# A two-layer block of four sequence mixers and a gated ffn: each engine's order set by another model of durations

## The chip, the core and the metric

The kernel runs on one core of a Trainium2 chip. The core has five engines that run side by side, each with an instruction stream of its own that it works through strictly in order: TensorE (PE, matrix multiplication into PSUM; PEld is its loading of weights), VectorE (DVE), ScalarE (ACT), GpSimd (POOL) and SyncE (SP, which here only issues DMAs). An instruction that needs another engine's result waits on a semaphore, and everything behind it on its own engine waits with it. The metric is device time in microseconds, the median of several executions.

## The reference

Two layers over 512 latent tokens and 256 context tokens of width 1024, in fp32. In each layer the tokens are normed and modulated (shift and scale computed from a vector `c` by `mod_w`), projected by `w_in` (3,232 columns), passed through four mixers of 256 columns each, projected by `w_out`, added, normed and modulated again, and passed through a gated ffn of width 2816. The last layer leaves out what only the context's output needs.

```
mod = split(silu(c) @ mod_w[i] + mod_b[i], 6)            # also for c_ctx
h   = modulate(x, norm_mix_g[i], mod[0], mod[1])         # rms norm * (1 + scale) + shift
pa, pb, pc, pd = split(h @ w_in[i])                       # both for x and ctx
oa = rwkv7(pa)      # delta rule: S = S*w + (S a) b^T + v k^T, two directions, 4 heads of 64
ob = diff_attention(pb)   # softmax(q1 k1) - lam * softmax(q2 k2), 4 heads
oc = gla(pc)        # gated linear attention in chunks of 64, two directions, 4 heads
od = gqa(pd)        # 4 query heads on 2 key heads, rope
x  = x + mod[2] * (concat(oa, ob, oc, od) @ w_out[i])
u, g = split(modulate(x, norm_ffn_g[i], mod[3], mod[4]) @ w_up[i])
x  = x + mod[5] * ((silu(conv3(g)) * u) @ w_down[i])
```

## The kernel before

Activations lie as [feature, token] tiles in 30 slabs of SBUF; all matmuls write slices of one PSUM tile named `pst`, so nearly every PE row reads `pst`. Fp32 operands of the large matmuls are split into a rounded part and a rest, and a product is three matmuls: L377 (ACT) rounds, L378 (POOL) subtracts, L387 and L703 multiply (L387 with the weights as the stationary side, giving [feature, token]; L703 with the activations as the stationary side, giving [token, feature]). `projections` (L709) makes all blocks of `w_in` through these two. Every matmul of a projection is independent of the mixers, whose inputs it makes.

The gated linear attention (`gla`, L1100) of one direction takes the cumulated gates (L1114, L1122, L1148, with sums along the tokens as matmuls at L427, the shared helper for transposes and constant products), the scores inside a chunk (L1163), a mask (L1181), the state's products L1186, and the outputs L1197 and L1200; its end on POOL is L1225. The delta rule (`rwkv`, L1260) prepares decays (L1345 to L1376, with L1389 on PE after L1366 on DVE), inverts small triangles (L1418, L1420 on DVE), and runs its chain of chunks (L1545 to L1663). The attentions follow with scores and softmax (L937 to L970; L859 turns the rotated queries).

The modulation is not done on PE alone: `mod_first` (L446) spreads layer 0's shift and scale over PE, DVE (L470) and POOL with ACT (L474, L475), and `mod_part` (L483) does the other 80 blocks of the two layers as 320 products with a sum on DVE (L495), woven into the mixers of layer 0 and into its ffn. A norm takes the mean square (L550), an inverse root by integer steps and three Newton steps on DVE (L400 to L407), a broadcast (L558, L561 on PE), and the scaling L576 and shift L580, whose outputs are the first projections' operands.

The order is set in two steps. `weave` (L300) emits the streams (delta rule, gated linear attention, attentions, projections, modulation) by turns: each has a clock that advances by the number that it yields times a pace, and the stream that is behind goes first. This order of emission gives the instructions their priorities. The framework then fixes each engine's stream with a simulated clock: an engine that comes free takes, of the instructions whose inputs are ready on that clock, the one that was emitted earliest. What it takes for the duration of an instruction, and for the time at which another engine sees a result, so decides which instruction is "ready" when an engine comes free. The resulting streams are fixed in the program; nothing is reordered on the chip.

## Time and profile before

| | us |
|---|---|
| Three runs of the kernel before | 2450.39 median, 2445.48 to 2453.73 |
| Span of the profiled execution | 2445.8 |
| PE busy | 2211.0 (90%) |
| DVE busy | 1490.5 (61%) |
| POOL busy | 1047.3 (43%) |
| ACT busy | 937.5 (38%) |

The page gives no time of the profiled execution beside its span; the span is 4.6 us under the median of the three runs. The span falls into these stretches, by what runs in them: 0 to 92 us the first norm and modulation; 92 to 437 the projections and the gated linear attention of layer 0, with the preparation of the delta rule; 437 to 846 the rest of the delta rule, the attentions and `w_out`; 846 to 1454 the ffn of layer 0, up to 1098 with the modulation of layer 1 on DVE; 1454 to 1517 the norm of layer 1; 1517 to 1830 projections and gated linear attention of layer 1; 1830 to 2026 its delta rule and attentions; 2026 to the end `w_out` and ffn. The granted clock (PEclk) is a share of full speed, averaged over a stretch; it goes between two levels, 2.4 and 1.2 GHz, so that 0.90 in a stretch means that the lower one held a fifth of it.

### The profile page before, as it was taken

How to read it: one execution, taken by the hardware profiler on the slowest of the kernel's cores; microseconds unless marked ns; L12 is line 12 of the kernel's file. 1: busy time of each engine (PE TensorE's matmuls, PEld its weight loads, DVE VectorE, ACT ScalarE, POOL GpSimd, SP SyncE). 2: the span in 40 equal slices, each digit the busy share in tenths (PEclk: the TensorE clock that was granted, in tenths of full speed). 3: DMA queues.
4: the chain of work that ended last, by engine and by line, in shares of the span. 5: the costliest groups of instructions: out<-in, count | busy, mean ns of one | idle time of the engine just before them, and what ended most of it. 6: DMA issues, size and time to landing. Idle time of an engine off the chain costs nothing. (4 is left out here: it accounts for less than half of the span.)

```text
span 2445.8 us, 40328 instructions
## 1 busy us (share of the span) xinstructions
PE 2211.0 (90%) x15292; PEld 1881.8 (77%) x15292; DVE 1490.5 (61%) x3201; ACT 937.5 (38%) x1758; POOL 1047.3 (43%) x1001
## 2 busy tenths in 40 slices
PE   4879898789979998969999999997989889999999
PEld 4767687677857787858888888786878778888888
DVE  6997568678764499994222262367778874423223
ACT  3322222256546342212232344323256564533333
POOL 3442356334221253334343464346433413555556
PEclk9889888799979999989999999898889999999999
DMA  7443134433224334542211142125533232222324
GB/s 250 168 151 119 47 126 121 109 95 84 74 73 139 101 113 148 172 153 70 67 63 61 61 157 70 48 67 148 135 90 83 59 122 95 87 94 95 98 93 138
DMA packets 232434, 259.54 MB, mean 106 GB/s; under 512 B 90992, under 2 KB 174256, under 8 KB 232240
## 3 DMA queue, kind: packets, MB, share of 16 engines
q1 hardware_dynamic: 232240, 256.97, 33.8%
q8 instruction: 120, 1.97, 0.3%
q14 instruction: 74, 0.61, 0.1%
HBM read 210.74 MB, written 37.77 MB: 102 GB/s over the span
## 5 line engine op out<-in xcount | busy, mean ns | idle before, releaser
L387 PE MATMUL pst<-slab,slab 128*128 128x512 f32 (+1 forms) x6552 | 1255.3, 353 | 55.0 <-ACT slab L631 20.8
L387 PEld LDWEIGHTS pst<-slab,slab 128*128 128x128 f32 x6552 | 1065.0, 193 | 239.3 <-ACT slab L631 21.4
L378 POOL TENSOR_TENSOR slab<-slab,slab 128x512 fp32r<-128x512 f32 (+1 forms) x428 | 584.0, 1374 | 728.5 <-ACT slab L377 685.0
L377 ACT CAST slab<-slab 128x512 fp32r<-128x512 f32 (+1 forms) x428 | 257.8, 612 | 538.0 <-PE pst L387 397.5
L703 PE MATMUL pst<-slab,slab 128*128 128x256 f32 (+1 forms) x1872 | 261.8, 302 | 17.9 <-POOL slab L378 17.7
L703 PEld LDWEIGHTS pst<-slab,slab 128*128 128x128 f32 x1872 | 250.4, 205 | 27.8 <-POOL slab L378 19.5
L620 DVE SCALAR_TENSOR_TENSOR slab<-pst,pp,slab 128x511 f32<-128x511 f32 x66 | 41.5, 657 | 312.6 <-ACT slab L617 312.6
L495 DVE SCALAR_TENSOR_TENSOR slab<-slab,slab 128x512 bf16<-128x512 f32 x240 | 227.6, 948 | 6.9 <-DMA slab<-in_modw_dram 0.8
L427 PE MATMUL pst<-cst,slab 128*128 128x128 f32 (+1 forms) x968 | 166.5, 305 | 60.0 <-POOL slab L1148 16.6
L427 PEld LDWEIGHTS pst<-cst,slab 128*128 128x128 f32 (+1 forms) x968 | 121.0, 153 | 88.0 <-DVE slab L859 20.0
L1545 PE MATMUL pst<-slab,slab 128*128 128x128 f32 (+5 forms) x1376 | 162.1, 278 | 9.1 <-DVE slab L1599 4.8
L651 DVE SCALAR_TENSOR_TENSOR slab<-pst,fgate,slab 128x512 f32<-128x512 f32 (+1 forms) x144 | 88.0, 629 | 127.5 <-PE pst L387 127.4
L1545 PEld LDWEIGHTS pst<-slab,slab 128*128 128x128 f32 (+3 forms) x1376 | 135.1, 176 | 29.8 <-issue 14.4
L940 DVE TENSOR_REDUCE mx<-pst 128x1 f32<-128x768 f32 (+1 forms) x120 | 100.2, 846 | 43.3 <-PE pst L937 20.6
L942 ACT ACTIVATE slab<-pst,mx 128x768 f32<-128x768 f32 (+1 forms) x120 | 97.9, 817 | 50.9 <-DVE mx L940 50.1
L632 POOL TENSOR_TENSOR slab<-slab,slab 128x768 fp32r<-128x768 f32 (+1 forms) x44 | 71.2, 1618 | 97.9 <-ACT slab L631 94.4
L626 ACT ACTIVATE slab<-slab 128x768 f32<-128x768 f32 (+1 forms) x44 | 32.4, 737 | 144.2 <-DVE slab L622 144.2
L495 DVE SCALAR_TENSOR_TENSOR slab<-slab 128x512 bf16<-128x512 f32 x80 | 73.5, 918 | 2.3
L1577 POOL TENSOR_TENSOR slab<-slab,pc 128x256 f32<-128x256 f32 x48 | 34.3, 727 | 87.6 <-PE pst L1545 16.0
L953 ACT ACTIVATE slab<-slab,r 128x768 f32<-128x768 f32 (+1 forms) x80 | 67.7, 853 | 8.7 <-DVE r L952 8.1
L970 PE MATMUL pst<-slab,slab 128*64 128x128 f32 x816 | 64.7, 291 | 3.8 <-ACT slab L422 1.7
L631 ACT CAST slab<-slab 128x768 fp32r<-128x768 f32 (+1 forms) x44 | 32.0, 728 | 92.1 <-DVE slab L628 92.0
(309 smaller groups left out, 2689.7 us busy)
## 6 DMA issues: line engine op xcount, KB each, us to landing
slab<-in_wup_dram SPq DMA_DIRECT2D x88, 512.0 KB, 3.4
slab<-in_modw_dram SPq DMA_DIRECT2D x160, 256.0 KB, 2.6
slab<-in_wdn_dram SPq DMA_DIRECT2D x48, 512.0 KB, 3.4
slab<-in_win_dram SPq DMA_DIRECT2D x46, 512.0 KB, 3.6
slab<-in_modw_dram SPq DMA_DIRECT2D x16, 512.0 KB, 7.0
slab<-in_wout_dram SPq DMA_DIRECT2D x16, 512.0 KB, 3.5
slab<-in_xT_dram SPq DMA_DIRECT2D x16, 384.0 KB, 5.7
kb<-slab SPq DMA_DIRECT2D x8, 768.0 KB, 4.2
```

The lines of the kernel that those rows point to most:

```text
L377: nc.scalar.copy(out=w[0], in_=st[:, k:k + q])
L378: nc.gpsimd.tensor_tensor(out=w[1], in0=st[:, k:k + q], in1=w[0].bitcast(F32), op=ALU.subtract)
L387: self.nc.tensor.matmul(ps[:, a:b], w[i][k][:, cols], x[j][k][:, a:b], start=(k == 0 and q == 0), stop=(k == nk - 1 and q == 2))
L427: self.nc.tensor.transpose(out, a.bitcast(F32) if a.dtype != F32 else a, self.c["ident"])
L495: nc.vector.scalar_tensor_tensor(out=junk, in0=w, scalar=1.0, in1=self.sc[s][:, e * hd:(e + 1) * hd], op0=ALU.mult, op1=ALU.mult, accum_ou ...
L632: nc.gpsimd.tensor_tensor(out=HL[:, 1, :n], in0=th[:, :n], in1=HL[:, 0, :n].bitcast(F32), op=ALU.subtract)
L651: nc.vector.scalar_tensor_tensor(out=x[m][:, a:b], in0=ps[:, a:b], scalar=gate[:, m, s:s + 1], in1=x[m][:, a:b], op0=ALU.mult, op1=ALU.add)
L703: self.nc.tensor.matmul(ps[:, :n], h[i][k][:, t * P:(t + 1) * P], w[j][k], start=(k == 0 and q == 0), stop=(k == KD - 1 and q == 2))
L940: nc.vector.tensor_reduce(out=mx, in_=sv, axis=AX.XY, op=ALU.max, negate=True)
L942: nc.scalar.activation(out=p[m][:, a:].rearrange("p (e c) -> p e c", e=2 - a // hb), in_=sv, func=AF.Exp, bias=mx, accum_out=lsum[:, m:m + 1])
L953: nc.scalar.activation(out=p[0][:, a:], in_=p[0][:, a:], func=AF.Copy, scale=r[:, 0:1])
L1545: mm = lambda o, a, b, pos: nc.tensor.matmul(o, a, b, start=True, stop=True, tile_position=pos)
```

## The change

One line changes in the code; the rest of the diff removes comments and docstrings.

```
-    with tile.TileContext(nc) as tc:
+    with tile.TileContext(nc, schedule_with_timeline_sim=True) as tc:
         tile_hybrid_block(tc, A, out)
```

The scheduler's clock then runs on a detailed model of the timeline (what an instruction takes on its engine, and when its result is seen by others) instead of a short table of durations. Every instruction is the same in number, shape and address: 12,488 on PE, 2,869 on DVE, 1,632 on ACT, 1,006 on POOL and 1,073 on SP by the program. Only their order on each engine differs. On PE the two ffn stretches keep their order; the stretches with projections and mixers do not.

The first place is PE in the second direction of the gated linear attention of layer 0. `slab_19_126` to `slab_24_131` are the attention's own tiles; `slab_1_96` to `slab_4_99` and `slab_34` to `slab_41` are operands of the projections. Before:

```order
L387 MATMUL pst<-slab_41_364,slab_4_99 128x512
L387 MATMUL pst<-slab_41_364,slab_4_99 128x256
L1186 MATMUL pst<-slab_19_126,slab_20_127 64x256 x4
L387 MATMUL pst<-slab_34_218,slab_4_99 128x512
L1197 MATMUL pst<-slab_24_131,slab_19_126 64x64 x4
L1200 MATMUL pst<-slab_23_130,slab_19_126 64x64 x4
```

After, the same steps:

```order
L703 MATMUL pst<-slab_4_99,slab_35_236 128x256 x3
L1163 MATMUL pst<-slab_24_131,slab_16_119 32x64 x48
L1186 MATMUL pst<-slab_19_126,slab_20_127 64x256 x2
L703 MATMUL pst<-slab_1_96,slab_36_259 128x256 x3
L703 MATMUL pst<-slab_1_96,slab_37_283 128x256 x3
L703 MATMUL pst<-slab_4_99,slab_34_218 128x256 x3
L703 MATMUL pst<-slab_4_99,slab_35_236 128x256 x3
L703 MATMUL pst<-slab_1_96,slab_36_259 128x256 x3
L703 MATMUL pst<-slab_1_96,slab_37_283 128x256 x3
L1197 MATMUL pst<-slab_24_131,slab_19_126 64x64 x4
L1186 MATMUL pst<-slab_21_128,slab_20_127 64x256 x2
L703 MATMUL pst<-slab_1_96,slab_34_218 128x256
```

The L1186 of this direction stood four in a row between projections at L387, and its L1197 and L1200 followed behind one more matmul. Now it is split into two pairs with eighteen matmuls of L703 between them, and those projections, which stood behind the whole direction, stand ahead of its outputs.

The second place is DVE in the first norm of layer 0: `r` and `t` are the inverse root's tiles, `slab_33_197` at L558 the broadcast that the norm goes on with, and the L470 the modulation's products with their sum into `mod_77`. Before:

```order
L405 TENSOR_TENSOR t_31_182<-r_181 128x6
L406 TENSOR_TENSOR t_31_182<-t_31_182,t_32_183 128x6
L407 SCALAR_TENSOR_TENSOR r_181<-t_31_182,r_181 128x6
L558 TENSOR_TENSOR slab_33_197<-cst,r_181 128x512
L558 TENSOR_TENSOR slab_33_197<-cst,r_181 128x256
L470 SCALAR_TENSOR_TENSOR slab_5_100,mod_77<-slab_17_124,slab_14_113 128x1024
L470 SCALAR_TENSOR_TENSOR slab_5_100,mod_77<-slab_17_124,slab_15_114 128x1024
L576 SCALAR_TENSOR_TENSOR slab_33_197<-slab_8_103,gs_167,slab_33_197 128x512
```

After, with the same Newton steps:

```order
L476 TENSOR_SCALAR mod_77<-mod_77,pp 128x2 x2
L470 SCALAR_TENSOR_TENSOR slab_5_100,mod_77<-slab_21_128,slab_14_113 128x1024
L405 TENSOR_TENSOR t_31_182<-r_181 128x6
L534 SCALAR_TENSOR_TENSOR gs_167<-mod_77,pp 128x2
L470 SCALAR_TENSOR_TENSOR slab_5_100,mod_77<-slab_21_128,slab_15_114 128x1024
L406 TENSOR_TENSOR t_31_182<-t_31_182,t_32_183 128x6
L476 TENSOR_SCALAR mod_77<-mod_77,pp 128x2
L470 SCALAR_TENSOR_TENSOR slab_5_100,mod_77<-slab_24_131,slab_14_113 128x1024
L407 SCALAR_TENSOR_TENSOR r_181<-t_31_182,r_181 128x6
L470 SCALAR_TENSOR_TENSOR slab_5_100,mod_77<-slab_24_131,slab_15_114 128x1024
L873 TENSOR_TENSOR lm_3402<-rows_381 128x64
L405 TENSOR_TENSOR t_31_182<-r_181 128x6
```

Before, L405 to L407 ran without a break up to the broadcast L558, and the L470s stood behind it. Now L470, L476 and L534 stand between the Newton steps; L558 comes further down, and eight L470 more than before stand ahead of it.

The third place is POOL near the end of the gated linear attention of layer 0, ahead of the splits L378 of the weights that L703 takes. L788 copies pieces of projections, L1225 gates the attention's output, L1369 and L1355 belong to the delta rule. Before:

```order
L1225 TENSOR_TENSOR slab_33_197<-slab_33_197,slab_25_132 128x256 x6
L788 TENSOR_TENSOR slab_7_102<-slab_17_124 128x128
L1369 TENSOR_TENSOR slab_23_130<-slab_23_130,slab_16_119 128x768
L1355 COPY pc_56_2045<-slab_21_128 128x12
L788 TENSOR_TENSOR slab_7_102<-slab_17_124 128x128
L378 TENSOR_TENSOR slab_2_97<-slab_7_102,slab_1_96 128x512
L378 TENSOR_TENSOR slab_2_97<-slab_7_102,slab_2_97 128x512
L378 TENSOR_TENSOR slab_3_98<-slab_5_100,slab_3_98 128x512
```

After:

```order
L1369 TENSOR_TENSOR slab_23_130<-slab_23_130,slab_16_119 128x768
L378 TENSOR_TENSOR slab_4_99<-slab_6_101,slab_4_99 128x512
L378 TENSOR_TENSOR slab_1_96<-slab_6_101,slab_1_96 128x512
L378 TENSOR_TENSOR slab_2_97<-slab_7_102,slab_1_96 128x512
L788 TENSOR_TENSOR slab_6_101<-slab_14_113 128x256
L378 TENSOR_TENSOR slab_2_97<-slab_7_102,slab_2_97 128x512
L1225 TENSOR_TENSOR slab_33_197<-slab_33_197,slab_25_132 128x256 x6
L788 TENSOR_TENSOR slab_6_101<-slab_24_131 128x256
```

Before, the six L1225 stood ahead of these L378. Now they stand behind them, and the first two L378 of the upper block (`slab_2_97`) stand further up still.

## Rows read from the trace of the kernel before

**Rows 1.** The page, section 1: busy us, share of the span, instructions.

```profile
PE 2211.0 (90%) x15292; PEld 1881.8 (77%) x15292; DVE 1490.5 (61%) x3201; ACT 937.5 (38%) x1758; POOL 1047.3 (43%) x1001
```

**Rows 2.** Windows: stretch, length; PE, PEld, DVE, ACT, POOL busy; PEclk, DMA, GB/s.

```profile
0.00:92.00 92.00, 52.59 (x196) 44.56 (x196) 70.34 (x133) 35.69 (x62) 39.13 (x25) 0.94 0.58 211
92.00:182.00 90.00, 73.84 (x446) 65.76 (x446) 85.71 (x179) 25.66 (x43) 41.88 (x28) 0.87 0.52 171
182.00:437.00 255.00, 224.71 (x1873) 190.97 (x1874) 176.21 (x397) 67.69 (x132) 119.19 (x109) 0.88 0.34 104
437.00:490.00 53.00, 35.47 (x235) 30.50 (x233) 38.20 (x103) 15.58 (x34) 18.23 (x38) 0.71 0.41 107
490.00:846.00 356.00, 323.92 (x2844) 268.11 (x2844) 236.50 (x602) 191.54 (x413) 102.85 (x154) 0.95 0.31 89
846.00:1098.00 252.00, 215.25 (x1155) 182.57 (x1155) 244.34 (x504) 68.37 (x105) 97.95 (x59) 0.93 0.46 153
1098.00:1454.00 356.00, 356.00 (x2059) 312.17 (x2059) 123.84 (x182) 109.50 (x170) 161.06 (x115) 1.00 0.25 80
...
1517.00:1727.00 210.00, 185.03 (x1561) 156.12 (x1559) 126.46 (x253) 71.94 (x133) 109.03 (x99) 0.91 0.30 90
1727.00:1830.00 103.00, 92.33 (x700) 79.92 (x700) 73.45 (x195) 39.63 (x86) 37.36 (x63) 0.82 0.43 108
1830.00:2026.00 196.00, 180.70 (x1813) 148.40 (x1812) 150.56 (x375) 124.59 (x252) 62.08 (x106) 0.97 0.31 88
```

**Rows 3.** TensorE's waits: us in total, times, the longest.

```profile
PE pst L703 <- POOL slab L378: 17.7, 8, 4.5
PE pst L427 <- POOL slab L1148: 16.6, 4, 8.0
PE pst L427 <- DVE slab L859: 16.5, 9, 8.5
PE pst L1389 <- DVE slab L1366: 14.1, 2, 8.8
...
PE pst L1122 <- DVE slab L1114: 9.9, 1, 9.9
...
PE pst L1186 <- DVE slab L1174: 7.2, 1, 7.2
```

**Rows 4.** Timeline of TensorE, 182 to 277 us: start, us, instruction, idle before.

```profile
187.56 1.54 PE L427 MATMUL pst<-cst,slab 128*128 128x128 f32 x6 [7.96 <-POOL slab L1148]
...
202.98 0.68 PE L1197 MATMUL pst<-slab,slab 64*64 64x64 f32 x8
...
273.55 1.12 PE L1186 MATMUL pst<-slab,slab 128*64 128x256 f32 x4 [7.25 <-DVE slab L1174]
...
275.32 1.11 PE L1197 MATMUL pst<-slab,slab 64*64 64x64 f32 x8
```

**Rows 5.** The page, section 5: one group of matmuls, busy us, mean ns.

```profile
L703 PE MATMUL pst<-slab,slab 128*128 128x256 f32 (+1 forms) x1872 | 261.8, 302 | 17.9 <-POOL slab L378 17.7
```

**Rows 6.** Timeline of POOL, 316 to 333 us.

```profile
318.41 5.38 POOL L1225 TENSOR_TENSOR slab<-slab,slab 128x256 f32<-128x256 f32 x6 [1.73 <-DVE slab L1224]
```

**Rows 7.** Timeline of DVE, 33 to 43 us.

```profile
33.39 1.03 DVE L558 TENSOR_TENSOR slab<-cst,r 128x512 f32<-128x512 f32 x2
34.33 1.22 DVE L470 SCALAR_TENSOR_TENSOR slab<-slab,slab 128x1024 bf16<-128x1024 f32 x1
...
39.13 3.39 DVE L470 SCALAR_TENSOR_TENSOR slab<-slab,slab 128x1024 bf16<-128x1024 f32 x1
```

**Rows 8.** Timeline of POOL, 33 to 45 us.

```profile
39.03 5.69 POOL L474 TENSOR_TENSOR slab<-slab,slab 128x1024 f32<-128x1024 f32 x2 [7.29 <-ACT slab L475]
```

**Rows 9.** Line L495 alone: durations, least, median, most.

```profile
L495 DVE SCALAR_TENSOR_TENSOR slab<-slab,slab x240: 660/692/2223, 86.2 to 1105.6; 128x512 bf16<-128x512 f32 x120
```

**Rows 10.** DVE by lines, 846 to 1098 us: busy us, mean ns.

```profile
L495 DVE SCALAR_TENSOR_TENSOR slab<-slab,slab 128x512 bf16<-128x512 f32 x140 | 133.8, 956 | 4.7 <-DMA slab<-in_modw_dram 0.8
L495 DVE SCALAR_TENSOR_TENSOR slab<-slab 128x512 bf16<-128x512 f32 x48 | 43.9, 914 | 1.5
```

## The prediction

> **What bounds the kernel now.** I read the page's first section first: TensorE is busy 90% of the span, DVE 61% [rows 1]. A kernel with one engine at 90% is bound by that engine and by what keeps it idle, so the next view is the table of windows, one row per stage: its length less PE's busy time is PE's idle time, and PEclk says how much of the stretch ran at the lower clock. The reader is to see three kinds of stage [rows 2]. The ffn of 1098 to 1454 us is saturated (356.00 busy of 356, clock 1.00): nothing is to be had there, and PE's order does not change in it. In 846 to 1098 PE is busy 215.25 of 252 but DVE 244.34: there DVE is the bound, and its own work sets the length. In the projections with the mixers of both layers neither is full: 92 to 437 leaves PE idle 16.2 + 30.3 = 46.5 us, 1517 to 1830 leaves 25.0 + 10.7 = 35.7, together 82.2, and those stretches have clocks of 0.87, 0.88, 0.91 and 0.82. Then I read PE's waits by what ended them: in these stages they are few and long, each a step of the gated linear attention or of the delta rule's preparation that another engine finishes late [rows 3]. In the timeline such a wait stands before one instruction, 7.96 us at 187.56 and 7.25 us at 273.55 [rows 4], while the projections, which wait for none of it, lie further down PE's stream. What follows a wait is slow too: eight L1197 took 0.68 us at 202.98 in a stretch without idle time, and the same eight 1.11 us at 275.32, just behind the wait of 7.25, which is the lower of the two clock levels against the higher [rows 4].
>
> **What the change does, part by part.** It removes and adds no instruction. The terms are what its order does at each wait.
>
> *Gated linear attention, both layers.* The new order puts projections ahead of PE's waiting instruction. Summing the trace's own durations of what is newly ahead of it, it is 9.7 us of PE work at L1122 (wait 9.9), 10.4 at the first L427 behind L1148 (8.0) and 55.7 at the second L1186 (7.2). In the first place shown in the order, eighteen L703 at 261.8 / 1872 = 0.14 us [rows 5], 2.5 us, stand between its two pairs alone; the rest stands further up. The waits of these kinds are 9.9 + 16.6 + 7.2 = 33.7 [rows 3].
>
> *L703 behind L378.* POOL's L378 was late since POOL did the mixers' work first: the six L1225 take 5.38 us [rows 6]. The order takes POOL work of 12.8, 13.2 and 3.4 us away from ahead of the L378 at three of the eight waits; I count two thirds of 17.7, 11.8 [rows 3].
>
> *L1389 behind L1366.* Before the two waits 31.7 and 19.7 us of projections are put: 14.1 [rows 3].
>
> Together 59.6 of the 82.2 us. All of it is the upper end, and nothing is the lower: the work put ahead takes operands that L377 and L378 have to make earlier, and PSUM slices that have to be emptied earlier, which no row of before shows. What is late next is the same pair ACT and POOL, in waits of up to 4.5 us [rows 3]. I take 60%, 36 us, near the upper end because what is put ahead (9.7 to 55.7 us) is longer than each wait.
>
> *Clock.* If the stretches ran at full clock, each would save at most (1 - PEclk) times its length: 0.13 x 90 = 11.7, 0.12 x 255 = 30.6, 0.09 x 210 = 18.9, 0.18 x 103 = 18.5, in sum 79.7 [rows 2]. PE was busy for some 0.85 of it or more, so 68 is what the lower clock costs in busy time. As PE loses the clock where it waits, I give back the same share as of the idle time, 36 / 82.2 = 0.44: 30 us. Ends: 0 and 68.
>
> *Start, 0 to 92 us.* DVE is busy 70.34 us and PE idle 39.4 [rows 2]. Before, L558 followed the Newton chain and the L470s came behind it [rows 7]. Now eight more L470 stand ahead of L558, and all later norm steps and the first matmuls are queued behind them on DVE: 8 x 1.22 = 9.8 us. That is no gain anywhere by itself, but the same L470s no longer stand between the later L576 and L580, so at best twice as much comes back there, a net -9.8. The other end: beside POOL's L474 (5.69 us for two, from 39.03 [rows 8]) one L470 took 3.39 [rows 7]; if all eight do, 8 x 3.39 = 27. I take +6, near the clean row, with a third of it covered by PE's idle time.
>
> The Trainium skill says why, in "SBUF — State Buffer", section "Who interferes with whom": a DVE instruction with two inputs in SBUF and a GpSimd instruction that reads SBUF exclude each other, the second waiting out the whole of the first. The rows agree: L470 1.22 alone and 3.39 beside L474. The rule speaks against this change, which draws the L470s forward to where the L474s run; by it the start would cost 27 in place of 6, and the whole gain would be 21 us smaller, about 2411.
>
> *437 to 490, 490 to 846, 1830 to 2026.* DVE gets eight or nine pairs L1418 and L1420 ahead of L859 and of the delta rule's L1599, and PE gets 4.5 to 6 us of filler at the same waits (L859's are 16.5 in all [rows 3]). I put these at 0, with 10 us either way, which is about two of the longest waits there (8.5).
>
> *846 to 1098.* DVE's order puts nine L495 ahead of an L622 and seven ahead of an L651 that PE waits for, and four fewer later. DVE is full here, so what PE loses early it finds again when DVE has done its 133.8 + 43.9 us of L495 [rows 10]: 0. Ends: four fewer at 0.96 are -4; sixteen more at 0.956 are +15 if none is repaid.
>
> Sum: -36 - 30 + 6 = -60 on the span of 2445.8, 2386; the profiled span is 4.6 us under the median of the runs, so the time is **2390**.
>
> **The rivals.**
>
> *A. The sum above*, 2390. With the haircut between 35% and 85% and the start from 0 to +15 it goes from 2360 to 2425.
>
> *B. Nothing is lost on the way.* All 82.2 us of idle time and all 68 of the clock come back: 2450 - 150 + 6 = 2306. For it: the work put ahead is two to eight times as long as most waits. Against it: no order can fill 82.2 when waits named in [rows 3] make up only 59.6.
>
> *C. The filler moves the waits.* PE takes the projections earlier, waits for their operands (L703 behind L378 has eight waits of up to 4.5 us: 8 x 4.5 = 36, as much as was won [rows 3]), and comes to the same mixer steps later. The clock does not come back either, as PE waits as often as before. Then the start's 6 remains or is repaid: 2440 to 2460. For it: POOL's L378 is paced by ACT's L377, not by the order. Against it: POOL is busy only 119.19 of 255 us in the stretch [rows 2].
>
> *D. Slower by DVE's order.* DVE works in order, and the new order puts modulation products ahead of what PE waits for: eight L470 ahead of L558 (9.8), eight L495 ahead of L733 at 133 us, nine ahead of L622 and seven ahead of L651, two more ahead of the L558 of the first ffn's norm: 26 x 0.956 = 24.9 at the mean of rows 10, together 34.7. If none of it is repaid and the mixers give a quarter of 36 + 30, 16, the time is 2450 + 35 - 16 = 2469, 2470 in round figures. It decides once the mixers give back less than 35 us. For it: an L495 alone takes 0.692 at the median and 2.223 at the most [rows 9], so the wait behind it can double where POOL works. Against it: in 846 to 1098 the bound is DVE's total, which is unchanged.
>
> That the change does nothing is excluded: on PE, DVE and POOL a large part of the order is another.
>
> **How the numbers follow.** A 0.56, B 0.08, C 0.13, D 0.23. A difference under 0.3% (7.4 us: 2443 to 2458) is about what a measurement of this kernel cannot tell from none. A and B are faster; of C's 0.13 I put 0.03 on faster, 0.07 on same and 0.03 on slower; D is slower. So faster 0.67, same 0.07, slower 0.26. The range goes from 2345, under A's own 2360 towards B, to 2465, into D: outside are B and the upper half of D.
>
> **What would show it.** Step by step in the profile after: the waits L1122 on L1114, L427 on L1148, L1186 on L1174 and L1389 on L1366 go from 47.8 to under 20 us, and L703 on L378 does not grow over 18; PEclk of the two projection stages rises to 0.93 or more, and their lengths shrink together by some 65; the L558 of the start begins 6 to 10 us later than 33.39. C is right if those waits go and others of the same sum stand in their place; D if 0 to 182 and 846 to 1098 are together over 25 us longer. The prediction is wrong in its mechanism if the mixers' stages do not get shorter, or if the gain lies in the ffn, where PE's order is as before.

## The result, and the profile after

The changed kernel takes 2470.83 us (median of 5 runs, 2467.02 to 2476.57) against 2448.93 before (5 runs): a ratio of 1.0087, 95% interval 1.0060 to 1.0114. It is slower by about 22 us, where 60 less were forecast, and outside the range. The time is that of rival D to within 1 us, but D's mechanism is not what the runs show.

TensorE is busy 4 us less than before [rows 1], so the 23 us that the span grew are idle time, of which there is 27 us more:

```profile
PE 2207.0 (89%) x15292; PEld 1880.9 (76%) x15292; DVE 1515.0 (61%) x3201; ACT 938.5 (38%) x1758; POOL 1062.0 (43%) x1001
```

The next rows are the windows of the changed kernel (the columns of [rows 2]), with the bounds moved so that a row holds about the work of its row in [rows 2]:

```profile
92.00:178.00 86.00, 74.55 (x468) 66.35 (x466) 84.09 (x181) 27.79 (x48) 38.16 (x26) 0.94 0.53 172
178.00:428.00 250.00, 217.81 (x1873) 186.25 (x1874) 181.70 (x371) 68.89 (x134) 122.33 (x111) 0.91 0.34 102
428.00:851.00 423.00, 368.13 (x3072) 305.91 (x3071) 282.68 (x723) 207.90 (x445) 126.69 (x192) 0.89 0.33 89
851.00:1103.00 252.00, 215.86 (x1167) 184.00 (x1167) 243.75 (x497) 68.10 (x107) 100.71 (x60) 0.91 0.49 153
...
1527.00:1738.00 211.00, 190.61 (x1596) 160.31 (x1595) 129.45 (x249) 72.67 (x134) 110.27 (x99) 0.92 0.32 93
1738.00:1838.00 100.00, 83.08 (x629) 72.24 (x629) 73.65 (x194) 36.82 (x80) 36.38 (x60) 0.80 0.42 104
1838.00:2050.00 212.00, 195.43 (x1864) 158.84 (x1863) 154.76 (x382) 128.79 (x259) 63.33 (x108) 0.95 0.30 83
```

The reader is to see two things. In the stages with projections and gated linear attention (92 to 428, 1527 to 1838), where 59.6 of 82.2 us of idle time were to go, the idle time is 11.5 + 32.2 + 20.4 + 16.9 = 81.0: nothing is gone. And the stages that were put at zero are longer: 428 to 851 is 423 us where the same work took 409 (53 + 356 in [rows 2]), and 1838 to 2050 is 212 against 196 (the bound ahead of it is uncertain by some us, so the table below goes by instructions).

A sharper cut, which the experiments use: seven parts of the program, at seams that the table's order has on every engine. When TensorE ends the last matmul of each part:

| Part | before, us | after, us | change of its length |
|---|---|---|---|
| 0: first norm and modulation | 90 | 98 | +8 |
| 1: to layer 0's last projection | 454 | 454 | -8 |
| 2: rest of its delta rule, attentions | 776 | 781 | +5 |
| 3: `w_out`, ffn, norm of layer 1 | 1478 | 1488 | +5 |
| 4: to layer 1's last projection | 1777 | 1785 | -2 |
| 5: rest of its delta rule, attentions | 2026 | 2046 | +12 |
| 6: `w_out`, ffn | 2443 | 2466 | +3 |

By windows over these parts, the growth of part 2 is busy time of TensorE (274.9 to 280.4 us), and that of part 5 is busy and idle time in like shares (227.4 to 233.9 busy, 21.6 to 27.1 idle); the granted clocks are 0.89 and 0.91 for 0.90 and 0.93. A column of such differences comes from one trace each, and traces differ without a change of order: part 4 in the table's order takes 300 us in the traces of the kernel before, of e5, e9 and e10, and 293 to 294 in those of e2, e6, e7, e11 and e17; part 5 in the table's order takes 250 us in the kernel before and in e4, and 257 in e3. A change under some 7 us in this table is not to be put down to the order; for that there are the runs below.

TensorE's waits after (the columns of [rows 3]):

```profile
PE pst L561 <- DVE slab L558: 36.9, 4, 23.1
...
PE pst L427 <- DVE slab L859: 17.9, 3, 7.6
PE pst L427 <- ACT slab L942: 14.6, 13, 3.3
...
PE pst L1389 <- ACT slab L1395: 9.9, 3, 5.0
PE pst L703 <- POOL slab L378: 9.1, 5, 4.4
PE pst L703 <- DVE slab L751: 7.7, 1, 7.7
...
PE pst L703 <- ACT slab L779: 6.8, 1, 6.8
...
PE pst L1122 <- DVE slab L1114: 6.2, 1, 6.2
PE pst L387 <- DVE slab L751: 6.0, 1, 6.0
...
PE pst L1389 <- DVE slab L1366: 3.8, 1, 3.8
...
PE pst L427 <- POOL slab L1148: 3.1, 1, 3.1
```

The waits that the prediction named are indeed small: L1122, L427 behind L1148 and L1389 behind L1366 were 9.9, 16.6 and 14.1 [rows 3] and are 6.2, 3.1 and 3.8; L1186 behind L1174 (7.2) is gone, and L703 behind L378 went from 17.7 to 9.1. In their place stand waits that before were not there at all or short: L703 and L387 behind L751 (7.7 + 6.0), L703 behind L779 (6.8), L1389 behind L1395 (9.9; 0.2 before). L751 and L779 are the evacuations of the projections' own results from PSUM, that is, the instructions by which DVE and ScalarE empty the slices. The longest group of all, L561 behind L558, is that of the norms (36.9 us, 11.0 before); it lies in the parts 0, 3 and 6.

At the start DVE and POOL show what the norm waited for:

```profile
31.58 14.48 POOL L474 TENSOR_TENSOR slab<-slab,slab 128x1024 f32<-128x1024 f32 x5 [0.69 <-DVE slab L434]
34.90 3.38 DVE L470 SCALAR_TENSOR_TENSOR slab<-slab,slab 128x1024 bf16<-128x1024 f32 x1
...
38.21 2.29 DVE L400 TENSOR_SCALAR t<-ms 128x6 int32<-128x6 int32 x1
40.42 0.16 DVE L403 TENSOR_SCALAR t<-ms 128x6 f32<-128x6 f32 x1
40.49 3.37 DVE L470 SCALAR_TENSOR_TENSOR slab<-slab,slab 128x1024 bf16<-128x1024 f32 x1
...
43.79 2.29 DVE L401 TENSOR_SCALAR r<-t 128x6 int32<-128x6 int32 x1
...
52.96 1.03 DVE L558 TENSOR_TENSOR slab<-cst,r 128x512 f32<-128x512 f32 x2
```

Two L470 of 3.4 us and two steps of the inverse root, L400 and L401, of 2.29 run here beside POOL's L474 (the like step between them, L403, takes 0.16); behind the end of the L474, at 46.06, four more L470 take 1.21 to 1.23 each. L558 begins at 52.96 in place of 33.39 [rows 7], 19.6 later and not 6 to 10.

### The profile page after: what moved, and what is told of

It is laid out like the page before. It is cut to its first block, busy times and chain, and to the rows that moved or that the text cites. A ratio compares the mean times of both kernels' runs of the same rounds, so it can differ in the third digit from the quotient of the medians.

```text
span 2469.0 us, 40361 instructions
## 1 busy us (share of the span) xinstructions
PE 2207.0 (89%) x15292; PEld 1880.9 (76%) x15292; DVE 1515.0 (61%) x3201; ACT 938.5 (38%) x1758; POOL 1062.0 (43%) x1001
## 5 line engine op out<-in xcount | busy, mean ns | idle before, releaser
L387 PE MATMUL pst<-slab,slab 128*128 128x512 f32 (+1 forms) x6552 | 1240.1, 351 | 56.2 <-ACT slab L631 18.2
L387 PEld LDWEIGHTS pst<-slab,slab 128*128 128x128 f32 x6552 | 1059.4, 192 | 232.0 <-ACT slab L631 18.8
L378 POOL TENSOR_TENSOR slab<-slab,slab 128x512 fp32r<-128x512 f32 (+1 forms) x428 | 584.6, 1376 | 788.7 <-ACT slab L377 739.6
L703 PE MATMUL pst<-slab,slab 128*128 128x256 f32 (+1 forms) x1872 | 264.9, 302 | 25.2 <-POOL slab L378 9.1
L703 PEld LDWEIGHTS pst<-slab,slab 128*128 128x128 f32 x1872 | 251.4, 205 | 41.1 <-issue 11.0
L495 DVE SCALAR_TENSOR_TENSOR slab<-slab,slab 128x512 bf16<-128x512 f32 x240 | 238.9, 995 | 5.2
L427 PE MATMUL pst<-cst,slab 128*128 128x128 f32 (+1 forms) x968 | 165.8, 306 | 55.6 <-DVE slab L859 17.9
L427 PEld LDWEIGHTS pst<-cst,slab 128*128 128x128 f32 (+1 forms) x968 | 121.3, 154 | 85.1 <-ACT slab L942 20.3
L1545 PE MATMUL pst<-slab,slab 128*128 128x128 f32 (+4 forms) x1376 | 170.6, 284 | 11.5 <-DMA slab<-scrout 6.4
L1545 PEld LDWEIGHTS pst<-slab,slab 128*128 128x128 f32 (+3 forms) x1376 | 143.8, 181 | 32.4 <-issue 10.7
L632 POOL TENSOR_TENSOR slab<-slab,slab 128x768 fp32r<-128x768 f32 (+1 forms) x44 | 71.9, 1634 | 41.4 <-ACT slab L631 36.9
L495 DVE SCALAR_TENSOR_TENSOR slab<-slab 128x512 bf16<-128x512 f32 x80 | 73.3, 916 | 2.0
L970 PEld LDWEIGHTS pst<-slab,slab 128*64 128x64 f32 x816 | 48.8, 147 | 20.3 <-DVE slab L424 6.1
L934 PE MATMUL pst<-slab,slab 128*128 128x384 f32 (+1 forms) x144 | 53.7, 421 | 11.5 <-ACT slab L942 4.8
```

The source lines that it names most:

```text
L378: nc.gpsimd.tensor_tensor(out=w[1], in0=st[:, k:k + q], in1=w[0].bitcast(F32), op=ALU.subtract)
L387: self.nc.tensor.matmul(ps[:, a:b], w[i][k][:, cols], x[j][k][:, a:b], start=(k == 0 and q == 0), stop=(k == nk - 1 and q == 2))
L427: self.nc.tensor.transpose(out, a.bitcast(F32) if a.dtype != F32 else a, self.c["ident"])
L495: nc.vector.scalar_tensor_tensor(out=junk, in0=w, scalar=1.0, in1=self.sc[s][:, e * hd:(e + 1) * hd], op0=ALU.mult, op1=ALU.mult, accum_ou ...
L632: nc.gpsimd.tensor_tensor(out=HL[:, 1, :n], in0=th[:, :n], in1=HL[:, 0, :n].bitcast(F32), op=ALU.subtract)
L703: self.nc.tensor.matmul(ps[:, :n], h[i][k][:, t * P:(t + 1) * P], w[j][k], start=(k == 0 and q == 0), stop=(k == KD - 1 and q == 2))
```

## The experiments

All seven parts can be given either order. The program is recorded twice, once by each model, to read both orders; in a third recording every engine's instructions are chained in the wanted order (an edge that only keeps order and adds no wait on the chip), part by part:

```
+PARTS = (2, 5)        # parts that take the timeline model's order
+    cuts = [last(0), last(1, 3), last(1), last(2), last(3, 3), last(3)]
+    part = lambda n: sum(at[n] > c for c in cuts)
+    def key(n):
+        p = part(n)
+        return p, rank[p in PARTS][n]          # rank[0]: the table's order, rank[1]: the model's
+            for a, b in zip(r, r[1:]):         # r: one engine's instructions by key
+                tc.add_manual_dep(ins[b], a, mybir.DependencyInfo(NoSync, DATA))
```

With no part chosen the order is that of the kernel before: e17, which chooses none, has in its trace the instructions of all five engines in that order, but for the block on TensorE that it moves. Lines of these kernels stand 9 further down (9 to 13 in the later ones): L868 is L859 of the kernel before. All were timed in 5 rounds beside the kernel before.

**e1, all parts** (`PARTS = (0, 1, 2, 3, 4, 5, 6)`). Expected: 

> The program is cut into seven parts at seams that the table's order has on every engine (end of the first norm; last projection of layer 0; end of its mixers; end of its ffn; the same of layer 1; the rest). Each part takes the timeline model's order, but nothing crosses a seam. If the loss lies inside the parts, the time is that of the changed kernel, 2465 to 2475 us; if it lies in what the model pulls across the seams, 2450 to 2460.

Measured: ratio 1.0133 (1.0115 to 1.0151), 2479.6 us, 32 above the kernel before. The loss lies inside the parts, and what the model pulls across the seams does not cost but gives back some 10 us.

**e2, delta rule and attentions** (`PARTS = (2, 5)`). Expected: 

> Only the parts with the delta rule's chain and the attentions (454 to 776 and 1777 to 2026 us of the kernel before) take the timeline model's order, the rest keeps the table's. By the theory that the loss is in these parts (their ends move by 5 and 12 us in the trace after): 2462 to 2470. By the rival of the prediction that DVE's modulation products are the loss, which these parts hold hardly any of: within 4 us of 2449.

Measured: 1.0127 (1.0104 to 1.0150), 31 us. These two parts alone are as slow as all seven, and slower than expected. Rival D falls: not one of its L495 is in them.

**e3, projections and gated linear attention** (`PARTS = (1, 4)`). Expected: 

> Only the parts with projections and gated linear attention (93 to 454 and 1477 to 1777 us) take the timeline model's order. By the prediction's sum 2390. By the trace after, in which the two parts are 8 and 2 us shorter: 2437 to 2443. By the theory that the filler only moves the waits: within 4 us of 2449.

Measured: 0.9978 (0.9962 to 0.9994), 5 us faster: the only version of the whole computation that beats both kernels. The waits of TensorE from 93 to 454 us in this run; there the kernel before had 9.9 (L1122), 9.7 (L427 behind L1148), 7.2 (L1186) and 14.1 us (L703 behind L378) of the kinds that were to go:

```profile
PE pst L712 <- DVE slab L734: 9.0, 3, 5.6
PE pst L396 <- DVE slab L760: 8.1, 2, 7.9
PE pst L712 <- DVE slab L760: 8.0, 1, 8.0
PE pst L712 <- ACT slab L788: 6.8, 1, 6.8
PE pst L1554 <- DMA slab<-scrout: 6.0, 1, 6.0
```

L734, L760 and L788 are the evacuations L725, L751 and L779 of the kernel before; their waits make 31.9 us, and to them come 6.0 behind a DMA of the delta rule. TensorE goes ahead to the projections, as forecast, fills the PSUM slices, and waits until DVE and ScalarE have emptied them. Why that is late, the longest of these waits shows (L1141 is the scan L1132 of the gates, L758 an evacuation like L760):

```profile
274.11 2.80 DVE L1141 TENSOR_TENSOR_SCAN slab<-reset,slab 128x768 f32<-128x768 bf16 x1 [5.02 <-POOL slab L1139]
...
276.83 1.11 DVE L758 SCALAR_TENSOR_TENSOR slab<-pst,pp,slab 128x511 f32<-128x511 f32 x2
...
279.61 1.62 PE L712 MATMUL pst<-slab,slab 128*128 128x256 f32 x6 [7.96 <-DVE slab L760]
```

DVE is idle for 5.02 us in front of the scan, which waits for POOL, and the evacuations stand behind the scan. DVE is not too slow here: the emptying has its place in DVE's order behind a step of the gated linear attention, the same kind of step that TensorE waited for before.

**e4, start and ffn of layer 0** (`PARTS = (0, 3)`). Expected: 

> Only the first norm (0 to 90 us) and the ffn of layer 0 with the norm of layer 1 (776 to 1478 us) take the timeline model's order; DVE's modulation products are moved there alone. By the rival of the prediction: 20 to 35 us slower, 2470 to 2484. By the trace after: the first norm ends 8 us later and the norm of layer 1 another 5, so 2454 to 2462, and nearer 2454 if the table's order of the projections finds the 8 again.

Measured: 1.0025 (1.0010 to 1.0040), 6 us. These parts hold all products that D put at 35, but for the eight L495 ahead of L733 (some 8 us of it), which lie in part 1 and so in e3. Together e2 to e4 make 31 - 5 + 6 = 32, what e1 has.

**e5, part 5 alone** (`PARTS = (5,)`). Expected: 

> Only the delta rule and attentions of layer 1 (1777 to 2026 us of the kernel before) take the timeline model's order. In the run of both such parts this one grew by 18 us and that of layer 0 by 10, so 2463 to 2469 if the two are independent; near 2449 if the loss needs layer 0's.

Measured: 1.0072 (1.0053 to 1.0091), 17.6 us. Layer 1 needs nothing of layer 0 for its loss.

**e7 and e8, the parts 2 and 5 cut once more behind their first 200 matmuls of the program.** Expected of the heads: 

> Of the delta rule and attentions of both layers only the first 200 matmuls' worth of program (some 50 to 60 us of each) takes the timeline model's order. Theory that the loss arises at the entrance, where inverses and rotation meet: 2465 to 2472, most of the 31 us of both whole parts. Rival that it arises at the end, where the attentions' last scores stand alone: 2449 to 2455.

Expected of what follows: 

> The rest of the same two parts, behind the first 200 matmuls, takes the timeline model's order; their heads keep the table's. Theory of the entrance: 2452 to 2460. Rival of the end: 2470 or more.

Measured: heads 1.0087 (1.0068 to 1.0106), 21 us; behind them 1.0095 (1.0072 to 1.0118), 23 us. Both theories hold half, and the halves do not add up to e2's 31. In e7 the loss is local: by the trace, after the first 55 us of TensorE's work in part 5 the run is some 13 us behind the kernel before, and as much at the end of the part; in part 2 it is some 6 and 4. In e8 what follows the head of part 5 takes 206.4 us in place of 195.0; TensorE's busy time there is 9.9 longer (189.39 for 179.46, at a clock of 0.93 for 0.96), so this loss is for the most part lower clock and not waits. The entrance of part 5 by windows, the kernel before and then e2 (its trace is of a run of 2468.8 us):

```profile
1777.00:1802.00 25.00, 20.07 (x114) 15.95 (x113) 18.16 (x50) 8.17 (x19) 10.03 (x22) 0.62 0.36 82
1802.00:1827.00 25.00, 23.65 (x218) 18.85 (x215) 17.05 (x36) 17.89 (x38) 7.76 (x14) 1.00 0.43 116
```

```profile
1780.00:1805.00 25.00, 10.74 (x55) 8.88 (x56) 14.05 (x42) 5.60 (x13) 9.25 (x23) 0.50 0.31 66
1805.00:1830.00 25.00, 22.25 (x161) 18.69 (x160) 14.07 (x27) 14.05 (x31) 4.04 (x8) 0.84 0.26 67
```

TensorE is busy 20.1 and 23.7 of 25 us before, 10.7 and 22.3 in e2, and the lower clock lasts longer (0.50 and 0.84 for 0.62 and 1.00). What it waits for, first in the kernel before:

```profile
1777.32 3.02 PE L1545 MATMUL pst<-slab,slab 64*64 64x64 f32 x24
...
1778.24 0.39 DVE L842 TENSOR_TENSOR slab<-slab,slab 128x128 f32<-128x128 f32 x1 [0.39 <-POOL slab L841]
1778.56 0.41 DVE L1418 TENSOR_TENSOR slab<-slab,slab 96x135 f32<-96x135 f32 x1
1778.89 0.28 DVE L846 TENSOR_TENSOR slab<-slab,rs0kda 128x128 f32<-128x128 f32 x1
...
1779.09 0.54 DVE L1420 TENSOR_TENSOR slab<-slab 96x135 f32<-96x135 f32 x1
```

and in e2:

```profile
1781.79 0.39 DVE L851 TENSOR_TENSOR slab<-slab 128x128 f32<-128x128 f32 x1 [1.02 <-POOL slab L850]
...
1785.43 1.12 PE L436 MATMUL pst<-cst,slab 128*128 128x128 f32 x4 [5.54 <-DVE slab L868]
...
1803.83 1.97 PE L436 MATMUL pst<-cst,slab 128*128 128x128 f32 x8 [7.92 <-DVE slab L868]
```

Before, DVE alternates a step of the attentions' rotation (L842, L846) with a step of the inverses (L1418, L1420), so that POOL's part of the rotation has time, and TensorE has 24 matmuls L1545 to run meanwhile. In e2's order the rotation runs in a row and waits for POOL (1.02 us in the row shown), the inverses come behind it, and TensorE's transposes L427 of what is rotated (here L436, behind L868) stand ahead of the L1545: TensorE waits 5.54 us. The second wait, of 7.92, is that of the late inverses: ScalarE's L867 needs the slab that holds them until they are stored, and waits 9.74 us for that DMA.

The changed kernel itself has only the second of these waits. There the model has pulled the same twelve transposes over the seam, to 1774 to 1777 us, where they wait for nothing; cutting at the seam puts them back. What its own trace shows is this:

```profile
1794.16 0.19 DVE L1420 TENSOR_TENSOR slab<-slab 96x31 f32<-96x31 f32 x1
...
1794.38 0.33 SPq L1422 DMA_DIRECT2D scrout<-slab  x1
...
1798.36 1.02 ACT L858 CAST slab<-slab 128x256 fp32r<-128x256 f32 x3 [9.21 <-DMA scrout<-slab]
...
1799.28 1.97 PE L427 MATMUL pst<-cst,slab 128*128 128x128 f32 x8 [7.38 <-DVE slab L859]
```

The inverses' last step ends at 1794.35, their store L1422 leaves SP's queue (SPq) at once, and when it is done ScalarE has been idle for 9.21 us and TensorE for 7.38; in the kernel before these transposes stand at 1792.15 without a wait. Counted by matmuls done, the changed kernel is 1 us behind the kernel before ahead of this wait, 8 us after it, and 17 us some 60 us further on. The next experiments all have e5's entrance or a piece of it, so they explain e2 and e5 better than the changed kernel.

**e6, the inverses first on DVE in part 5.** Expected: 

> As e5_part5, but on DVE the last 12 instructions of the triangles' inverses (L1418, L1420) stand at the head of the part, where the table's order has them, and not behind 25 instructions of the attentions' rotation (L842, L846, L859); all other engines keep the timeline model's order. Theory that the late inverses are the loss at the entrance (their DMA scrout leaves 14.5 us later and the delta rule's chain with it): 10 to 14 us less than e5_part5, 2451 to 2457. Rival that PE's order is (transposes L427 of the rotated queries ahead of twelve L1545): the rotation then comes 4 us later still, and the time is that of e5_part5 or up to 4 us more.

```
+        return p, p == 5 and n not in first, rank[p in PARTS][n]   # first: the inverses' instructions
```

Measured: 1.0101 (1.0079 to 1.0124), 7 us above e5. Moving the inverses alone does not help. The trace says why:

```profile
1781.80 0.19 DVE L1430 TENSOR_TENSOR slab<-slab 96x31 f32<-96x31 f32 x1
...
1799.99 0.58 SPq L1433 DMA_DIRECT2D scrout<-slab  x1
...
1804.17 1.02 ACT L867 CAST slab<-slab 128x256 fp32r<-128x256 f32 x3 [10.48 <-DMA scrout<-slab]
...
1805.09 1.97 PE L436 MATMUL pst<-cst,slab 128*128 128x128 f32 x8 [9.81 <-DVE slab L868]
```

The inverses end at 1782, but their store, L1433 (scrout), leaves SP's queue at 1800: it is 27th of the part there. The slab that it reads is the one that ScalarE wants next, and TensorE waits 9.81 us at the end of that row. This place in the queue costs only where the inverses are early: in e5 and in the changed kernel they end later, and the store leaves at once.

**e9, their store first on SP as well.** Expected: 

> As e6_part5_inverses_first, and on SP the store of the inverses (L1422, DMA scrout) stands at the head of the part too, where it was 27th; the table's order has it 7th. In e6 the inverses were done at 1782 us, yet this store left SP's queue at 1800, and until then ScalarE waited 10.5 us for its slab, DVE for ScalarE, and TensorE 9.8 us for DVE. Theory that SP's queue is what held it: 8 to 12 us less than e6, 2460 to 2464. Rival that TensorE's own order is the loss there: the time of e6, 2468 to 2476.

Measured: 1.0079 (1.0055 to 1.0102), 2463.95 us against 2472.65 of e6. The medians differ by 8.7 us, but the kernel before was 1.9 us faster beside e9 than beside e6, and by the ratios it is 5 us with intervals that overlap: less than the 8 to 12 that were expected, and e5's time again. Of the wait of 9.81 there is left (the trace is of a run of 2478.56 us):

```profile
1808.92 1.97 PE L436 MATMUL pst<-cst,slab 128*128 128x128 f32 x8 [0.85 <-DVE slab L868]
```

But the rotation, now behind the inverses, is later: the two waits on it ahead of that one are 8.36 and 4.39 us, where e5 has 5.94 and 0.22.

**e10, and twelve L1545 first on TensorE.** Expected: 

> As e9_store_first, and on TensorE the first twelve L1545 of the part stand ahead of the twelve transposes L427 of the rotated queries, as in the table's order, so that something is there to do while DVE rotates. Theory of TensorE's order: the wait before the transposes (8.6 us in e6) shrinks by the 3 us that these L1545 take, and the chain behind them starts 8 us earlier: 3 to 8 us less than e9. By SP's queue alone: within 3 us of e9.

```
+                r[i:i + 24] = r[i + 12:i + 24] + r[i:i + 12]     # TensorE, from the head of part 5
```

Measured: 1.0075 (1.0058 to 1.0093), that of e9. With all three undone the entrance still has these waits on the rotation:

```profile
1782.12 1.11 PE L436 MATMUL pst<-cst,slab 128*128 128x128 f32 x4 [5.41 <-DVE slab L868]
1787.49 1.97 PE L436 MATMUL pst<-cst,slab 128*128 128x128 f32 x8 [4.26 <-DVE slab L868]
```

With 2.11 and 0.85 behind them, TensorE's waits on L868 at the entrance are 12.6 us; they are 14.0 in e5, 18.8 in e6 and 13.6 in e9, against 2.6 in the kernel before. That goes with the times, 18, 18, 25 and 19 us above the kernel before in e10, e5, e6 and e9: each of these orders makes either the rotation or the inverses late on DVE.

**e17, one feature put into the kernel before: the transposes ahead of the L1545.** Expected: 

> The kernel before in the table's order, with one feature of the timeline model's: at the head of layer 1's delta rule and attentions (1777 us) TensorE's twelve transposes L427 of the rotated queries stand ahead of the twelve L1545. Theory that this order of TensorE is what costs at the entrance (13 us in e7): 2454 to 2460. Theory that it costs only the 3 us that the L1545 take there, while the rotation is late either way: 2447 to 2452.

Measured: 1.0032 (1.0013 to 1.0051), 8 us, by the interval 3 to 12: of the 13 that the entrance of part 5 loses in e7, TensorE's order costs some of it on its own. The trace cannot say how much: 25 us into part 5 it is 5.9 us behind the kernel before, but e3, with the table's order there, is 4.5 behind at the same matmul. In e10 the same order put right gave nothing. There the inverses stand ahead of the rotation and make it later, so the three are perhaps bound to each other, and only an alternation like the table's serves all; that is argued and not shown.

**e11 and e12, the modulation among layer 0's mixers made small.** These two kernels leave out 504 of the 512 columns of each of these products, so their sums are incomplete and their output is not that of the block; the orders are read from the whole program (`FULL[0]` is true then). Expected of the base, in the table's order: 

> The table's order throughout, but the modulation's products of layer 0 that lie among the mixers (L495, 128 of them) take 8 of their 512 columns, so that their sums are left incomplete; the order is that of the full size. This is the base of e12_small_products_gla: DVE loses about 110 of 266 busy us in the part, TensorE's waits on DVE shorten: 2420 to 2445.

Expected with part 1 in the model's order: 

> As e11_small_products, with the timeline model's order in the projections and gated linear attention of layer 0 (93 to 454 us). Theory that the gain of this order is eaten by DVE, where L495 stand ahead of the evacuations L725, L749 and L751 that the earlier projections wait for (25 us of new waits in e3): 15 to 30 us less than e11. Theory that the earlier projections wait for their evacuation whatever DVE does: within 6 us of e11, as the whole products gave 4.

```
+                    n = hd if li or FULL[0] else 8
-                    nc.vector.scalar_tensor_tensor(out=junk, in0=w, scalar=1.0, in1=self.sc[s][:, e * hd:(e + 1) * hd],
+                    nc.vector.scalar_tensor_tensor(out=junk[:, :n], in0=w[:, :n], scalar=1.0, in1=self.sc[s][:, e * hd:e * hd + n],
```

Measured: 0.9851 (0.9830 to 0.9873), 2412.8 us, and 0.9870 (0.9850 to 0.9889), 2413.7 us. The base is faster than expected (36 us), and the model's order gains nothing over it. So it is not the products ahead of the evacuations that eat the gain; with DVE relieved TensorE still waits as long as in e3 behind L751 (here L763), L779 (L791) and the delta rule's DMA (6.0 us):

```profile
PE pst L715 <- DVE slab L763: 8.0, 1, 8.0
PE pst L715 <- ACT slab L791: 6.8, 1, 6.8
```

**e13 to e16, the emission order.** The weave's paces for layer 1 are part of the kernel before, and they set what both models start from:

```
-    PACE = ((1.0, 0.7, 1.0, 1.0, 1.0, 1.0), (0.69, 0.7, 1.0, 0.6, 1.0, 1.15))
+    PACE = ((1.0, 0.7, 1.0, 1.0, 1.0, 1.0), (1.0, 0.7, 1.0, 1.0, 1.0, 1.0))
```

Expected, even paces by the table: 

> The kernel before with layer 1's paces of the streams set to those of layer 0 (delta rule 1.0 for 0.69, attentions 1.0 for 0.6): another order of emission for layer 1's mixers, ordered by the table. Base of e14_even_paces_model. Theory that the paces were set for the table's clock: slower than the kernel before, 2455 to 2475. Theory that they matter little: within 6 us of 2447.

By the model: 

> The changed kernel with the same even paces. Theory that the loss belongs to the timeline model's order whatever the emission: 20 to 26 us above e13, as the changed kernel stands above the one before. Theory that the loss of layer 1's delta rule and attentions (18 of the 31 us) comes of paces that suit the table alone: within 8 us of e13, or below it.

Middle paces (0.8, 0.7, 1.0, 0.8, 1.0, 1.0) by the table: 

> As e13, with paces between the two (delta rule and attentions of layer 1 at 0.8), ordered by the table. Paces set for the table: between the kernel before and e13. Else within 6 us of 2447.

By the model: 

> As e15, by the timeline model. Loss belongs to the model's order: 20 to 26 us above e15. Paces that suit the table alone: within 8 us of e15.

Measured against the kernel before: even 1.0088 (1.0063 to 1.0112) by the table and 1.0148 (1.0127 to 1.0169) by the model; middle 1.0060 (1.0037 to 1.0082) and 1.0097 (1.0074 to 1.0119). The table loses 22 and 15 us by other paces, so these suit it. The model stands above the table by 22 us at the kernel's paces, 15 at the even and 9 at the middle ones. Neither theory has it whole: a third to over half of the loss, by figures that are uncertain by some 6 us each, goes with an emission order that suits the table's clock, the rest stays with the model.

**e18, the attentions' pace alone, 0.8 under the model.** Expected: 

> The changed kernel with one pace of layer 1 other: the attentions at 0.8 in place of 0.6, so that their rotation is emitted later against the delta rule. If the emission order that suits the table is what costs the model in layer 1: 5 to 12 us less than the changed kernel, 2458 to 2466. If the model's order loses as such: 2467 to 2477.

Measured: 1.0112 (1.0088 to 1.0136), 2476.8 us, at the upper end of the changed kernel's. That one pace gives nothing back, as the second of the two theories expected.

## Why the prediction was wrong

**Gated linear attention, L1389 and L703 (36 us).** The waits named went as forecast: the first four kinds from 47.8 to 13.1 us, under the 20 that would show it. The step that failed is the haircut, "I take 60%, 36 us, near the upper end because what is put ahead (9.7 to 55.7 us) is longer than each wait". That length was no reason (and at L1122 it was not even so, 9.7 against 9.9): matmuls put ahead end in PSUM slices that have to be emptied, and their emptying did not come ahead with them; it stands on DVE and ScalarE behind the same chains. Parts 1 and 4 are 8 and 2 us shorter in the trace after, e3 is 5 faster, and the idle time of these stages went from 82.2 to 81.0. The lower end named in the same paragraph (operands and PSUM slices earlier, "which no row of before shows") was the likely one. Rival C, at 0.13, had it for these stages by its sign, others of much the same sum in their place (30.4 us of the new waits for 34.7 that went), but not by its reason: the wait on operands that it named, L703 behind L378, fell from 17.7 to 9.1. e12 shows that DVE's modulation is not needed for it.

**Clock (30 us).** It was tied to the idle time, at the same share. The clocks of the four windows are 0.94, 0.91, 0.92 and 0.80 for 0.87, 0.88, 0.91 and 0.82 [rows 2]. Layer 0 gained, about (0.94 - 0.87) x 86 + (0.91 - 0.88) x 250 = 13 us at full clock, though its idle time fell only from 46.5 to 43.6; layer 1 did not. And the parts 2 and 5, for which the prediction priced no clock, have 12 us more of busy time.

**Start (+6).** L558 came 19.6 us later, between the clean row's 9.8 and the other end of 27. The rule of the Trainium skill that the prediction quoted ("SBUF — State Buffer", section "Who interferes with whom") agrees with the two L470 of 3.4 us beside L474, but not all eight met it: together they took 14.7 us, and the rest of the 19.6 is small steps that took longer too. Part 1 made up for it (454 in both), and e4 prices the start and the ffn's start together at 6. The size of the step was wrong; that its worth came out right is luck.

**437 to 490, 490 to 846, 1830 to 2026 (0, 10 either way).** This is the second step that failed, and it set the sign. Parts 2 and 5 lose 17 us in the changed kernel and 31 when they alone are changed (e2), beyond the bound of 10. The prediction had seen pairs L1418 and L1420 put ahead of L859 and a few us of filler move, and called it even, with bounds from single waits. In the changed kernel 5 of the 17 us are idle time and 12 are busy time at a lower clock. The idle time has a cause that can be seen: in part 5 the inverses end late on DVE, their store and ScalarE's L858 with them, and TensorE waits 7.38 us where it waited for nothing. Why the clock is lower further on is not shown. In the kernels cut at the seams (e2, e5) the entrance is worse, since there the rotation also runs in a row and waits for POOL, with the transposes ahead of the L1545. What the prediction did not ask is what an alternation on DVE was good for: in the kernel before it gives POOL time for its part of the rotation and yet ends the inverses early. e6, e9 and e10 show that putting the inverses first, with their store and TensorE's order, only moves the wait to the rotation; that the alternation would bring the time back is argued, since no run restores it in the changed kernel. For the 10 or so behind the heads, in either part, no cause is shown.

**846 to 1098 (0).** Right: 252 us before and after.

**Rival D.** Its time is the measured one, by accident. Its place is not: e4 holds all of its products but those among the mixers and costs 6, and in e2, without its L495, the loss is whole. Its own sign is absent too: 0 to 178 and 851 to 1103 make 430 us, where 0 to 182 and 846 to 1098 made 434.

What stays open: how much of the loss in parts 2 and 5 belongs to the model's durations and how much to the emission order (e13 to e18 say that both have a share), and on which engine's order it hangs: no run gives these parts the model's order on one engine alone.

## What to carry to other kernels

Work put ahead of a wait on the bounding engine is a gain only if what it produces is taken away in time: look where the emptying of its results (here PSUM, by DVE and ScalarE) stands in those engines' orders before counting the wait as filled, and read the idle time of the stage, not the named waits. An order that alternates two chains on one engine can be there for other engines' sake; before calling a regrouping even, look at who works in the gaps (POOL and TensorE here). Who moves a chain has to move its DMA along: in e6 a store left 20 places behind held a slab for 18 us. A kernel that is cut at seams to find a loss has an order of its own at the seam, so what it shows has to be looked for in the changed kernel's trace as well. And a list scheduler's emission order and its clock suit each other: in this kernel the gap between the two models went from 22 to 9 us with the paces, so the paces have to be set again before the models can be compared.

## What the runs showed of the hardware

Steps of the inverse root on DVE, of one tensor input and 6 columns, took 2.29 us at 38.21 and 43.79 of the changed kernel, and a like one 0.16 at 40.42, all while POOL ran its L474 (31.58 to 46.06): even such a small instruction can take fourteen times as long there. The kernel before has it too (L400 1.57 us at 27.75). Relieving DVE of some 75 us among layer 0's mixers (its busy time from 93 to 422 us is 191 in e11; 266 from 93 to 454 in the kernel before) made the whole kernel 36 us faster, though DVE was busy no more than three quarters of that stretch.
